# The first two RMS norms of a one-core decoder step: the sum of squares by a stationary of ones, mean and root on every partition

## The chip, the core and the metric

The kernel runs on one core of a Trainium2 chip. The core has a matrix engine (PE, with its weight loads shown apart as PEld), a vector engine (DVE), a scalar engine (ACT), a general engine (POOL) and a queue for transfers (SP). Each works through its own instructions in order and waits on the others through semaphores. The metric is the device time of one execution in microseconds. The kernel before takes 1652.54 us, the median of 3 runs (1651.92 to 1653.86). The kernel keeps a matmul's contraction on the 128 partitions; results land in PSUM banks, all other data lie in SBUF.

## The reference

One layer of a hybrid decoder is computed for 256 prompt tokens and 32 sample tokens together (288 columns, D = 2048 features, 16 blocks of 128 on the partitions):

```
def rmsnorm(x, g):
    y = x32 * lax.rsqrt(jnp.mean(x32 * x32, axis=-1, keepdims=True) + RMS_EPS)
    return y * g

h = rmsnorm(x, norm_mix);  z = h @ w_in             # norm 1, then the input projections
x = x + mixer(z) @ w_out                            # RG-LRU branch and attention branch
x = x + conv_ffn(rmsnorm(x, norm_ffn))              # norm 2, then gate, up, conv, gelu, down
y = rmsnorm(x, norm_final)                          # norm 3
```

In the kernel the features are the partitions and the tokens the columns, so a norm's sum over features runs across partitions, and its root is one number for each column, needed on every partition.

## The kernel before

**Tiling and order.** Nearly all of the work is weight matrices of 128 x 128 against 288 token columns. `unit` (line 181) makes one output block of 128 features: it takes one to three weight tiles from `load_w`, eight 128 x 128 blocks in each, and for every block `mm3` (lines 177 to 179) issues three matmuls, high part by high part, high by low, low by high. A unit of two tiles is 48 matmuls. The program is written in the order in which it runs: no scheduler moves anything (the schedule is manual), and each engine gets its instructions in program order. `load_w` keeps three weight tiles split ahead: each split is an ACT copy that rounds (line 159) and a DVE subtraction (line 160), and there are three buffers for the parts and four for the raw tiles. Units write to one of two PSUM banks in turn (`psg`), so the first matmul of a unit waits until the unit two before it has been read out of its bank.

**The norms.** The scale of a token is applied after the matmul, on the way out of PSUM, so that the projections can begin before the root is known. Norm 1: squares are summed over the 16 blocks into `acc` (128 partitions x 288); then lines 407 to 426 interleave the norm with the first two units, `qx[0]` and `qx[1]`. Norm 2: `squares` on POOL fills `acc` during the output projection; lines 1121 to 1139 interleave the norm in the same way with the first gate unit `q0` and the first up unit `q1`. The steps of a norm are

- `rms_sum` (line 250): three matmuls with 128 columns of `acc` as the stationary and a single column of ones moving; the sums come out with the tokens on the partitions, one column for each 128 tokens;
- `rms_root` (lines 256 and 258): on DVE times 1/D plus eps, 128 x 3, and on POOL the power -1/2, 128 x 3;
- after one weight tile of the next unit, `rms_bcast` (line 266): three matmuls with a root column spread to 128 columns as the stationary and the identity moving, so that every partition gets the row of roots;
- `rms_rows` (line 271): ACT copies that row of 288 from PSUM to `rb`.

Then DVE multiplies the waiting PSUM banks by `rb`: in norm 1 `xr_out` (lines 378, 379) for `qx[0]`, four blocks of `kv[0]` (line 425) and `xr_out` for `qx[1]`; in norm 2 `ffn_gate` (lines 1084, 1085) for `q0` and, after the convolution (1095), `ffn_up` (1100) for `q1`. Behind the root on POOL stand, in norm 1, two DMA issues (427, 467) and in norm 2 the fills of `u` (1080, 1083). Norm 3, at the end, uses the same helpers and is not touched.

Of the kernel before, what the change touches and what calls it, by code (L numbers as in the profile page):

```python
# [9 lines left out]
F32 = mybir.dt.float32  # L10
# [4 lines left out]
ALU = mybir.AluOpType  # L15
# [3 lines left out]
P = 128  # L19
D = 2048  # L20
# [4 lines left out]
N = NP + NS  # L25
# [9 lines left out]
EPS = 1e-6  # L35
# [52 lines left out]
def body(ctx, tc, a, o):  # L88
    nc = tc.nc
    V, S, G, T = nc.vector, nc.scalar, nc.gpsimd, nc.tensor  # L90
# [5 lines left out]
    tmp = ctx.enter_context(tc.tile_pool(name="tmp", bufs=2))  # L96
    ps = ctx.enter_context(tc.tile_pool(name="ps", bufs=2, space=PSUM))

    def bank(tag, bufs):
        return lambda: ps.tile([P, 512], F32, tag=tag, name="ps_" + tag, bufs=bufs)  # L100

    psg, pss, pst, pso, psb = bank("g", 2), bank("s", 2), bank("t", 1), bank("o", 1), bank("b", 2)
# [78 lines left out]
    def unit(out, n, xh, xl):  # L181

        for i in range(n):
            wh, wl = load_w()
            for k in range(8):
                kk = 8 * i + k
                mm3(out, wh[:, k], wl[:, k], xh[:, kk], xl[:, kk], kk == 0, kk == 8 * n - 1)
            if i < n - 1:
                yield
# [20 lines left out]
    ones = cst.tile([P, P], F32, name="ones")  # L210
    V.memset(ones, 1.0)
    mhalf = cst.tile([P, 4], F32, name="mhalf")
# [30 lines left out]
    def new_acc():  # L243
        acc = tmp.tile([P, 384], F32, tag="cv", name="acc")
        V.memset(acc[:, N:], 0.0)
        return acc

    def rms_sum(q, acc, first, last):
        for tb in range(3):
            T.matmul(q[:, tb:tb + 1], acc[:, tb * P:(tb + 1) * P], ones[:, 0:1], start=first and tb == 0, stop=last,  # L250
                     skip_group_check=True)

    def rms_root(q):

        ms = tmp.tile([P, 4], F32, tag="ms", name="ms", bufs=1)
        V.tensor_scalar(ms[:, :3], q[:, :3], 1.0 / D, EPS, op0=ALU.mult, op1=ALU.add)
        rt = tmp.tile([P, 4], F32, tag="rt", name="rt", bufs=1)
        G.tensor_tensor(rt[:, :3], ms[:, :3], mhalf[:, :3], op=ALU.pow)
        return rt

    def rms_bcast(rt):

        q = pss()
        for tb in range(3):
            n = min(P, N - tb * P)
            T.matmul(q[:, tb * P:tb * P + n], rt[:, tb:tb + 1].to_broadcast([P, P]), ident[:, :n], start=True, stop=True)
        return q

    def rms_rows(q):
        rb = tmp.tile([P, N], F32, tag="rb", name="rb", bufs=1)  # L270
        S.activation(rb, q[:, :N], AF.Copy)
        return rb
# [10 lines left out]
    acc = new_acc()  # L283
# [80 lines left out]
    rb = None  # L364
# [12 lines left out]
    def xr_out(j, q):  # L377
        V.tensor_mul(xr[:, j, 3:3 + NP], q[:, :NP], rb[:, :NP])
        V.tensor_mul(xs[:, j, :, 3:], ptok(q[:, NP:N]), ptok(rb[:, NP:]))
# [27 lines left out]
    qn = pss()  # L407
# [4 lines left out]
    r_lam0()  # L412
    for _ in g:
        pass
    rms_sum(qn, acc, True, True)
    rt = rms_root(qn)
    g = unit(qx[1][:, :N], 2, hh, hl)
    next(g)
    qb = rms_bcast(rt)
    for _ in g:  # L420
        pass
    rb = rms_rows(qb)
    xr_out(0, qx[0])
    for j in range(4):
        V.tensor_mul(kv[0][:, j], kz[j][:, :N], rb)
# [630 lines left out]
    acc = new_acc()  # L1056
# [20 lines left out]
    def ffn_gate(f, qg):  # L1077
        u = tmp.tile([P, FW], F32, tag="sx", name="u", bufs=2)
        us = u[:, 2 + NP:].rearrange("p (b t) -> p b t", t=2 + TS)
        G.memset(u[:, 0:2], 0.0)  # L1080
        if 8 <= f < 8 + NB:
            nc.gpsimd.dma_start(o["win"][f - 8], a["win"][f - 8])
        G.tensor_copy(us[:, :, 0:2], fst[:, f].rearrange("p (b t) -> p b t", t=2))
        V.tensor_mul(u[:, 2:2 + NP], qg[:, :NP], rb[:, :NP])  # L1084
        V.tensor_mul(us[:, :, 2:], ptok(qg[:, NP:N]), ptok(rb[:, NP:]))  # L1085
        cv = tmp.tile([P, FW], F32, tag="cv", name="cv")
        S.activation(cv[:, :FC], u[:, 2:2 + FC], AF.Identity, scale=vcol(V_FW + 96, f), bias=vcol(V_FB, f))  # L1087
        G.tensor_copy(fco[:, f, 0:2], u[:, NP:NP + 2])  # L1088
        G.tensor_copy(fco[:, f, 2:18].rearrange("p (b t) -> p b t", t=2), us[:, :, TS:TS + 2])
        late.append(lambda: ffn_conv(f, u, cv))  # L1090
        return cv
# [32 lines left out]
    flush()  # L1124
    for _ in g:
        pass
    qn = pst()
    rms_sum(qn, acc, True, True)
    rt = rms_root(qn)
    q1 = psg()  # L1130
    g = unit(q1[:, :N], 2, h2h, h2l)
    next(g)
    qb = rms_bcast(rt)
    for _ in g:
        pass
    rb = rms_rows(qb)
    cv = ffn_gate(0, q0)
    flush()
    ffn_up(0, q1, cv)
# [13 lines left out]
    acc = new_acc()  # L1153
# [10 lines left out]
    qn = pst()  # L1164
    rms_sum(qn, acc, True, False)
    rms_sum(qn, ex, False, True)
    wake(psg(), 5)
    rt = rms_root(qn)
    q = rms_bcast(rt)
    rb = rms_rows(rms_bcast(rt))  # L1170

# [106 lines left out]
```

## Time and profile before

| what | value |
|---|---|
| median of 3 runs | 1652.54 us (1651.92 to 1653.86) |
| the profiled execution | 1652.34 us |
| its span, first to last instruction | 1650.6 us |
| PE busy | 1639.1 us, 99% |
| DVE, ACT, POOL busy | 994.5, 777.7, 201.4 us |

The span leaves 1.7 us of the profiled execution outside it. A busy PE is not a PE at its peak, since a matmul's end is modelled and overlaps the next; what counts on PE is the distance from one start to the next. The chain of waits follows the work that ended last back to the start.

### The profile page before, as it was taken

The page shows a single profiled execution, that of the slowest core. Times are in us where ns is not written, and L with a number is a line of the kernel's source. Part 1 is how long each engine was busy: PE and PEld are TensorE (multiplying, and loading weights), DVE is VectorE, ACT ScalarE, POOL GpSimd, SP SyncE. Part 2 cuts the span into 40 slices and gives each one's busy share as a digit, 9 for nine tenths or more (in the row PEclk, how much of TensorE's full clock was granted, in tenths as well). Part 3 has the DMA queues.
Part 4 walks back from the last instruction along what each step waited for, and adds up shares of the span by engine and source line. Part 5 has one row for each costly group of instructions (what it writes and reads, how often), then busy time and mean ns, then how long its engine had stood idle before and what let it go on. Part 6 is the DMA issues. An engine that isn't in the chain of part 4 may idle for free.

```text
span 1650.6 us, 31453 instructions
## 1 busy us (share of the span) xinstructions
PE 1639.1 (99%) x12738; PEld 1631.9 (99%) x12738; DVE 994.5 (60%) x1540; ACT 777.7 (47%) x1125; POOL 201.4 (12%) x406
## 2 busy tenths in 40 slices
PE   9999999999999999999999999999999999999997
PEld 9999999999999999999999999999999999999997
DVE  7777776776665555656555656444465556564443
ACT  6566464676754444434444444333344444443332
POOL 1341100421210002330010000000000000001111
PEclk9999999999999999999999999999999999999999
DMA  8655585555565555555576655555555555555553
GB/s 283 180 167 157 166 289 180 147 176 157 175 229 163 173 167 166 168 165 157 175 216 205 180 171 163 177 166 166 165 165 170 165 167 171 172 173 173 162 172 107
DMA packets 89298, 290.78 MB, mean 176 GB/s; under 512 B 10386, under 2 KB 20498, under 8 KB 89026
## 3 DMA queue, kind: packets, MB, share of 16 engines
q1 hardware_dynamic: 86114, 277.00, 55.3%
q0 software_dynamic: 1888, 10.32, 2.0%
q8 instruction: 100, 1.64, 0.4%
q10 hardware_dynamic: 1152, 1.45, 0.3%
q14 instruction: 44, 0.36, 0.1%
HBM read 284.02 MB, written 8.85 MB: 177 GB/s over the span
## 4 chain that ended last, share of the span: by engine, by line
PE 95%; issue 2%; DVE 1%; DMA 1%; POOL 0%; ACT 0%; SPq 0%; ACTq 0%; DVEq 0%; POOLq 0%
PE ps_g L177 30%; PE ps_g L179 30%; PE ps_g L178 30%; PE ps_b L607 1%; PE ps_o L843 0%; DMA kt<-in_slk_dram 0%; DVE wl L160 0%; PE ps_s L828 0%; PE ps_t L834 0%; PE ps_b L957 0%; DVE x L1175 0%; DMA raw<-in_wkc_dram 0%; PE ps_b L177 0%; PE ps_b L179 0%; PE ps_b L178 0%
## 5 line engine op out<-in xcount | busy, mean ns | idle before, releaser
L160 DVE TENSOR_TENSOR wl<-raw,wh 128x1024 fp32r<-128x1024 f32 (+1 forms) x496 | 619.1, 1249 | 463.9 <-ACT wh L159 462.6
L159 ACT ACTIVATE wh<-raw 128x1024 fp32r<-128x1024 f32 (+1 forms) x496 | 522.7, 1054 | 372.7 <-PE ps_g L178 284.3
L177 PE MATMUL ps_g<-h2h,wh 128*128 128x288 f32 x1536 | 450.3, 293 | 0.0
L178 PE MATMUL ps_g<-h2l,wh 128*128 128x288 f32 x1536 | 450.1, 293 | 0.0
L179 PE MATMUL ps_g<-h2h,wl 128*128 128x288 f32 x1536 | 449.4, 293 | 0.0
L177 PE MATMUL ps_g<-hh,wh 128*128 128x288 f32 x1024 | 304.2, 297 | 0.1
L178 PE MATMUL ps_g<-hl,wh 128*128 128x288 f32 x1024 | 300.3, 293 | 0.0
L179 PE MATMUL ps_g<-hh,wl 128*128 128x288 f32 x1024 | 299.8, 293 | 0.0
L179 PEld LDWEIGHTS ps_g<-h2h,wl 128*128 128x128 f32 x1536 | 288.8, 188 | 0.0
L178 PEld LDWEIGHTS ps_g<-h2l,wh 128*128 128x128 f32 x1536 | 288.3, 188 | 0.0
L177 PEld LDWEIGHTS ps_g<-h2h,wh 128*128 128x128 f32 x1536 | 288.3, 188 | 0.0
L177 PE MATMUL ps_g<-gh,wh 128*128 128x288 f32 x768 | 225.0, 293 | 0.0
L178 PE MATMUL ps_g<-gl,wh 128*128 128x288 f32 x768 | 225.0, 293 | 0.0
L179 PE MATMUL ps_g<-gh,wl 128*128 128x288 f32 x768 | 224.7, 293 | 0.0
L177 PEld LDWEIGHTS ps_g<-hh,wh 128*128 128x128 f32 x1024 | 192.3, 188 | 0.7 <-issue 0.4
L178 PEld LDWEIGHTS ps_g<-hl,wh 128*128 128x128 f32 x1024 | 192.3, 188 | 0.3
L179 PEld LDWEIGHTS ps_g<-hh,wl 128*128 128x128 f32 x1024 | 192.5, 188 | 0.0
L179 PEld LDWEIGHTS ps_g<-gh,wl 128*128 128x128 f32 x768 | 144.4, 188 | 0.0
L178 PEld LDWEIGHTS ps_g<-gl,wh 128*128 128x128 f32 x768 | 144.2, 188 | 0.0
L177 PEld LDWEIGHTS ps_g<-gh,wh 128*128 128x128 f32 x768 | 144.1, 188 | 0.0
L1088 POOL COPY fco<-u 128x2 f32<-128x2 f32 x48 | 8.8, 184 | 712.0 <-DVE u L1084 712.0
L1087 ACT ACTIVATE cv<-u,vec 128x304 f32<-128x304 f32 x48 | 30.8, 642 | 132.4 <-DVE u L1085 132.4
(327 smaller groups left out, 2016.4 us busy)
## 6 DMA issues: line engine op xcount, KB each, us to landing
raw<-in_wg_dram SPq DMA_DIRECT2D x96, 512.0 KB, 3.6
raw<-in_wu_dram SPq DMA_DIRECT2D x96, 512.0 KB, 4.1
raw<-in_wd_dram SPq DMA_DIRECT2D x96, 512.0 KB, 3.7
raw<-in_wga_dram SPq DMA_DIRECT2D x32, 512.0 KB, 3.8
raw<-in_wgb_dram SPq DMA_DIRECT2D x32, 512.0 KB, 3.6
raw<-in_wo_dram SPq DMA_DIRECT2D x32, 512.0 KB, 3.6
raw<-in_wxr_dram SPq DMA_DIRECT2D x16, 512.0 KB, 3.7
raw<-in_wgr_dram SPq DMA_DIRECT2D x16, 512.0 KB, 3.7
```

The costliest lines, as they stand in the source:

```text
L159: S.activation(hi, src, AF.Copy)
L160: eng.tensor_sub(lo, src, hi.bitcast(F32))
L177: T.matmul(out, wh, xh, start=first, stop=False)
L178: T.matmul(out, wh, xl, start=False, stop=False)
L179: T.matmul(out, wl, xh, start=False, stop=last)
L607: T.matmul(pc[:, 2 * k:2 * k + 272], w[:, l], f(x), start=lh == 0 and k == 0 and l == 0 and n == 0, stop=lh == 1 and k == 1 and l == 7 and ...
L1087: S.activation(cv[:, :FC], u[:, 2:2 + FC], AF.Identity, scale=vcol(V_FW + 96, f), bias=vcol(V_FB, f))
L1088: G.tensor_copy(fco[:, f, 0:2], u[:, NP:NP + 2])
```

## The change

A new helper, `rms_all`, takes the place of `rms_sum`, `rms_root`, `rms_bcast` and `rms_rows` in norms 1 and 2. One matmul has a 128 x 128 block of ones as the stationary and all of `acc` moving, 288 columns, so each partition receives the sum for every token. DVE then does times 1/D plus eps on 128 x 288 out of PSUM, and POOL takes the power on 128 x 288 straight into `rb`, with the exponent read from one column that is repeated.

```
+    def rms_all(q, acc):
+        T.matmul(q[:, :N], ones, acc[:, :N], start=True, stop=True)
+        ms = tmp.tile([P, N], F32, tag="th", name="msr")
+        V.tensor_scalar(ms, q[:, :N], 1.0 / D, EPS, op0=ALU.mult, op1=ALU.add)
+        rb = tmp.tile([P, N], F32, tag="rb", name="rb", bufs=1)
+        G.tensor_tensor(rb, ms, mhalf[:, 0:1].to_broadcast([P, N]), op=ALU.pow)
+        return rb
...
-    rms_sum(qn, acc, True, True)
-    rt = rms_root(qn)
+    rb = rms_all(qn, acc)
     g = unit(qx[1][:, :N], 2, hh, hl)
     next(g)
-    qb = rms_bcast(rt)
     for _ in g:
         pass
-    rb = rms_rows(qb)
     xr_out(0, qx[0])
...
-    qn = pst()
-    rms_sum(qn, acc, True, True)
-    rt = rms_root(qn)
+    rb = rms_all(pst(), acc)
     q1 = psg()
     g = unit(q1[:, :N], 2, h2h, h2l)
     next(g)
-    qb = rms_bcast(rt)
     for _ in g:
         pass
-    rb = rms_rows(qb)
     cv = ffn_gate(0, q0)
```

On PE in norm 1, between the units `qx[0]` and `qx[1]` (`ps_s` is the norm's bank, `ps_g` a unit's; a name with a number after "waits" is the engine's or transfer's semaphore):

```order
 L178 MATMUL ps_g<-hl,wh 128x288
 L179 MATMUL ps_g<-hh,wl 128x288
-L250 MATMUL ps_s<-ones,acc 128x1 [waits DVE_49]
-L250 MATMUL ps_s<-ones,acc 128x1 x2
+L263 MATMUL ps_s<-acc,ones 128x288 [waits DVE_49]
 L177 MATMUL ps_g<-hh,wh 128x288 [waits Activation_49]
 L178 MATMUL ps_g<-hl,wh 128x288
```

Three matmuls of one column became one of 288 columns. Half-way through `qx[1]`:

```order
 L178 MATMUL ps_g<-hl,wh 128x288
 L179 MATMUL ps_g<-hh,wl 128x288
-L266 MATMUL ps_s<-cs,rt 128x128 [waits DMAHW2_49,Pool_49]
-L266 MATMUL ps_s<-cs,rt 128x128
-L266 MATMUL ps_s<-cs,rt 128x32
 L177 MATMUL ps_g<-hh,wh 128x288 [waits Activation_49]
 L178 MATMUL ps_g<-hl,wh 128x288
```

The three matmuls that spread the roots are gone, and with them PE's own wait for POOL. On DVE in norm 1, before (`wl` are splits of coming weight tiles, `xr` and `kv` the read-outs):

```order
L256 TENSOR_SCALAR ms<-ps_s 128x3 [waits PE_49]
L160 TENSOR_TENSOR wl<-raw,wh 128x1024 [waits DMAHW5_49,Activation_49]
L160 TENSOR_TENSOR wl<-raw,wh 128x1024 [waits DMAHW6_49,PE_49,Activation_49]
L378 TENSOR_TENSOR xr<-ps_g,rb 128x256 [waits Activation_49]
L379 TENSOR_TENSOR xr<-ps_g,rb 128x8x4
L425 TENSOR_TENSOR kv_426<-ps_b,rb 128x288 x2
```

and after:

```order
L265 TENSOR_SCALAR msr<-ps_s 128x288 [waits PE_49]
L160 TENSOR_TENSOR wl<-raw,wh 128x1024 [waits DMAHW5_49,Activation_49]
L160 TENSOR_TENSOR wl<-raw,wh 128x1024 [waits DMAHW6_49,PE_49,Activation_49]
L387 TENSOR_TENSOR xr<-ps_g,rb 128x256 [waits Pool_49]
L388 TENSOR_TENSOR xr<-ps_g,rb 128x8x4
L431 TENSOR_TENSOR kv_426<-ps_b,rb 128x288 x2
```

The places are the same; the mean became 288 columns wide, and the first read-out now waits for POOL instead of ACT. Norm 2 reads alike on both engines, with `u` in the place of `xr`.

## Rows read from the trace of the kernel before

**Rows 1.** The page: busy time of each engine, share of the span, instructions

```profile
PE 1639.1 (99%) x12738; PEld 1631.9 (99%) x12738; DVE 994.5 (60%) x1540; ACT 777.7 (47%) x1125; POOL 201.4 (12%) x406
```

**Rows 2.** The page: the chain that ended last, shares of the span by engine

```profile
PE 95%; issue 2%; DVE 1%; DMA 1%; POOL 0%; ACT 0%; SPq 0%; ACTq 0%; DVEq 0%; POOLq 0%
```

**Rows 3.** Timeline, PE, norm 1: start us, us, engine, line, operation, tiles, shapes, count

```profile
37.75 0.72 PE L250 MATMUL ps_s<-ones,acc 128*128 128x1 f32 x6
...
38.55 0.30 PE L178 MATMUL ps_g<-hl,wh 128*128 128x288 f32 x1
...
41.58 0.75 PE L266 MATMUL ps_s<-cs,rt 128*128 128x128 f32 x6
...
42.39 0.29 PE L178 MATMUL ps_g<-hl,wh 128*128 128x288 f32 x1
...
45.42 0.29 PE L177 MATMUL ps_g<-hh,wh 128*128 128x288 f32 x1
```

**Rows 4.** Timeline, PE, in the attention stage: plain f32 matmuls 256 columns wide

```profile
452.69 0.60 PE L828 MATMUL ps_s<-kv,q_sb 128*128 128x256 f32 x2
...
453.26 0.29 PE L178 MATMUL ps_g<-hl,wh 128*128 128x288 f32 x1
```

**Rows 5.** Timeline, DVE, norm 1 (in brackets: idle before, and who ended it)

```profile
38.51 0.16 DVE L256 TENSOR_SCALAR ms<-ps_s 128x3 f32<-128x3 f32 x1 [0.78 <-PE ps_s L250]
...
42.79 1.23 DVE L160 TENSOR_TENSOR wl<-raw,wh 128x1024 fp32r<-128x1024 f32 x1 [2.61 <-ACT wh L159]
43.94 0.42 DVE L378 TENSOR_TENSOR xr<-ps_g,rb 128x256 f32<-128x256 f32 x1
44.27 0.18 DVE L379 TENSOR_TENSOR xr<-ps_g,rb 128x32 f32<-128x32 f32 x1
```

**Rows 6.** Timeline, ACT, norm 1: the copy of the roots

```profile
42.66 0.40 ACT L271 ACTIVATE rb<-ps_s 128x288 f32<-128x288 f32 x1
```

**Rows 7.** Timeline, DVE, norm 2

```profile
736.36 0.16 DVE L256 TENSOR_SCALAR ms<-ps_t 128x3 f32<-128x3 f32 x1 [1.47 <-PE ps_t L250]
...
741.73 0.42 DVE L1084 TENSOR_TENSOR u<-ps_g,rb 128x256 f32<-128x256 f32 x1
742.07 0.18 DVE L1085 TENSOR_TENSOR u<-ps_g,rb 128x32 f32<-128x32 f32 x1
...
744.04 0.45 DVE L1100 TENSOR_TENSOR t<-ps_g,rb 128x288 f32<-128x288 f32 x1
...
745.73 1.23 DVE L160 TENSOR_TENSOR wl<-raw,wh 128x1024 fp32r<-128x1024 f32 x1 [0.42 <-ACT wh L159]
```

**Rows 8.** Groups of POOL by line and shape: busy us, mean ns | idle before

```profile
L872 POOL TENSOR_TENSOR rest<-kt,k 128x512 f32<-128x512 f32 x32 | 38.6, 1206 | 123.3 <-ACT k L171 104.8 <-DVE k L174 12.8 <-DVE mx L799 2.2
...
L1050 POOL TENSOR_TENSOR m<-m,mA 128x288 f32<-128x288 f32 x16 | 12.9, 809 | 136.7 <-DVE m L1049 128.1 <-DVE acc L245 8.6
...
L258 POOL TENSOR_TENSOR rt<-ms,mhalf 128x3 f32<-128x3 f32 x3 | 2.6, 875 | 22.6 <-DVE ms L256 22.6
...
L767 POOL TENSOR_TENSOR pcs<-pcs,t 128x128 f32<-128x128 f32 x2 | 0.8, 400 | 34.0 <-DVE t L765 34.0
```

**Rows 9.** Timeline, POOL, norm 1 (first row) and norm 2

```profile
38.83 0.85 POOL L258 TENSOR_TENSOR rt<-ms,mhalf 128x3 f32<-128x3 f32 x1 [8.99 <-DVE ms L256]
...
736.60 0.89 POOL L258 TENSOR_TENSOR rt<-ms,mhalf 128x3 f32<-128x3 f32 x1 [4.15 <-DVE ms L256]
...
737.50 0.58 POOL L1083 COPY u<-fst 128x16 f32<-128x16 f32 x1
...
742.50 0.20 POOL L1083 COPY u<-fst 128x16 f32<-128x16 f32 x1
```

**Rows 10.** Timeline, PE: the same matmul at the start and at the end

```profile
1.07 4.21 PE L277 MATMUL ps_g<-ones 128*128 128x128 f32 x18 [1.07 <-DVE mhalf L213]
...
1638.79 1.36 PE L277 MATMUL ps_g<-ones 128*128 128x128 f32 x10
```

**Rows 11.** Stretches: us, busy of PE, PEld, DVE, ACT, POOL, granted clock, DMA share, GB/s

```profile
1642.00:1650.00 8.00, 0.00 (x0) 0.00 (x0) 3.60 (x7) 0.11 (x1) 2.30 (x3) 0.70 0.83 295
```

## The prediction

> **What bounds the kernel now.** I read the page first, then the chain of waits, then the two norms engine by engine. PE is busy for 99% of the span [rows 1] and is 95% of the chain that ended last [rows 2]: the kernel is a single file of matmuls. So an edit is worth what it takes out of PE's file, less any hole it opens there; work on DVE, ACT and POOL is free as long as PE doesn't wait for it. In the timeline of PE around norm 1 the reader is to see starts, not durations: 23 matmuls lie between the starts at 42.39 and 45.42 us, so one costs PE 0.132 us [rows 3].
>
> PE does not wait in either norm today. The first read-out that needs the roots starts at 43.94 us and its second half ends at 44.27 + 0.18 = 44.45 us [rows 5]; the unit that needs the bank it empties starts at 45.42 us [rows 3]. There is about 1 us to spare.
>
> **What comes out of PE's file.** `rms_sum` costs 38.55 - 37.75 = 0.80 us from its first start to the start of the second unit matmul behind it, with one unit matmul in between: 0.80 - 0.13 = 0.67 us for six instructions (each plain f32 matmul is two). `rms_bcast` in the same way: 42.39 - 41.58 - 0.13 = 0.68 us [rows 3]. Together 1.35 us a norm.
>
> **What goes in.** One plain f32 matmul 288 columns wide. Before has none of that width with these operands; the nearest is the pair 256 columns wide in the attention stage: 453.26 - 452.69 - 0.13 = 0.44 us [rows 4], so 0.44 x 288/256 = 0.50 us. Its bounds are 0.44 and the 0.67 of the six instructions. PE gains 1.35 - 0.50 = 0.85 us a norm (0.68 to 0.91), 1.7 us for both. That is 0.1% of the kernel, and it is all that the change can gain: ACT's copy of 0.40 us [rows 6] lies beside PE's work, as does the wider mean on DVE.
>
> **What it opens: the chain to the roots.** In norm 1 the sum would start on PE at 37.75 us as before and take 0.50. The mean started 38.51 - 37.75 = 0.76 us after the six instructions' first start [rows 3, 5], so it now starts at about 38.4 us. Its 128 x 288 out of PSUM costs about 0.45 us (the nearest DVE pass of that width from PSUM [rows 7]) in place of 0.16 [rows 5], so it ends at about 38.9; POOL's power started 0.16 us after the mean's end (38.51 + 0.16 = 38.67 to 38.83 [rows 5, 9]), so the power starts at about 39.0 us. Call its time D. Then comes the read-out, 0.51 us as before, and a tenth for the semaphore. PE needs the bank at 45.42 - 0.85 = 44.57 us. So **the hole in PE is D - 5.0 us**, none if D is below 5.0. Norm 2 has the same steps over the same 48 matmuls (mean at 736.36, read-out 741.73 to 742.25 [rows 7]), so the same hole.
>
> **What is D?** The trace has no power 288 columns wide, so it is bounded from both sides.
>
> - Below: other two-operand POOL passes take 809 ns at 288 columns [rows 8]. If a power is no dearer than these, D = 0.81 us.
> - Above: the power itself takes 875 ns for three columns [rows 8], in all three places alike (0.85 and 0.89 us in the first two [rows 9]). Lines through the other passes, 400 ns at 128 columns, 809 at 288, 1206 at 512, leave 0.08 to 0.30 us at three columns; I take 0.2. So 0.675 us are the power's own, 225 ns a column if all of it goes by columns: D = 0.2 + 288 x 0.225 = 65 us.
> - Between: part of the 0.675 may be paid once. The row just behind the power shows such a cost: the same 16-column copy takes 0.58 us there and 0.20 us on its next turn [rows 9]. With 0.38 us paid once, 0.295 us are left, 98 ns a column: D = 0.2 + 0.38 + 28.2 = 28.8 us.
>
> I take 29 us: the row with the power in it is nearer than any row of another operation, and the one-off is shown beside it, if on another instruction.
>
> What is queued behind: on DVE all read-outs and the next weight split, on POOL two transfers and two fills, which the read-outs' own shift covers. PE is held by the bank alone; the two tiles of the unit that it waits to start are split ahead of the waiting read-out on DVE.
>
> **The clock.** After a hole PE may restart slower. At the start of the kernel 18 of the warm-up instructions take 4.21 us, at the end ten take 1.36 [rows 10]: 4.21 - 18 x 0.136 = 1.8 us lost, roughly the 1.2 level against 2.4 GHz. With no matmul at all the granted clock averages 0.70 [rows 11], so it does fall in a hole. I add 1.8 us a hole, 0 to 1.8 being the bounds.
>
> **Sum**, against the profiled execution of 1652.3 us (the median of the runs is 0.2 above it): -1.7 for PE, +2 x 24 for the holes, +3.6 for the clock: 1652.3 - 1.7 + 48 + 3.6 = **1702 us**.
>
> **Rivals.**
>
> - *The cover holds* (not slower). D is under 5 us, so the power ends before PE wants the bank. Then the read-out waits for the second weight split in front of it, which ends at 42.79 + 1.23 = 44.0 us [rows 5] and moves up with PE, and all that is left is PE's gain: 1650.6 us, "same". It decides at 5.0/288 = 17 ns a column; up to D = 7.5 us the time stays within 0.2%. For it: the other passes' 809 ns. Against it: 875 ns for three columns, which would have to be a fixed cost almost whole. The Trainium skill speaks for this rival (GPSIMD Engine Reference, "Elementwise — side-by-side cycle accounting"): it states about 2.6 cycles an element for an elementwise pass with two operands, measured on an add; by that rule the power would take an estimated 0.6 us plus its dispatch, and the time would be 1650.6 us. The rows of add and multiply agree with it; the row of the power, 875 ns for three columns, does not fit it.
> - *The full price.* All 225 ns go by columns, D = 65 us: 1650.6 + 2 x 60 + 3.6 = 1774 us. For it: the three powers cost the same though the engine did different work before each. Against: the copy's one-off.
> - *A second wait behind the first.* DVE holds the later weight splits behind the read-out, so PE could run dry again after it restarts. In norm 2 the first split behind it ends at 745.73 + 1.23 = 746.96, 4.7 us after the read-out's end at 742.25 [rows 7], and PE then has a unit of 48 x 0.132 = 6.3 us in hand. Price nothing; 1702 stands. It would decide at 1.6 us more on DVE or ACT.
> - *Faster.* PE would have to lose more than 3.3 us of work; both norms hold only 2.7 us of it.
>
> **How the numbers follow.** About 0.2% (3.3 us) is what a measurement of this kernel can tell from no change. The cover holds: 0.30. The forecast, a column price from about 50 to 160 ns: 0.47. The full price: 0.20. Faster: 0.03, for something unseen. So slower 0.67, same 0.30, faster 0.03. The range runs from the case in which the cover holds, 1650, to the full price, 1774; beyond it lie a power dearer than its own row and a faster kernel. The likeliest case's own range is from half its column price (D = 15: 1650.6 + 20 + 3.6 = 1674) to the full price, 1674 to 1774.
>
> **What would show it.** In the profile after, POOL's row for the power 128 x 288 decides: under 5 us the cover holds, about 29 us is my forecast, about 65 the full price. PE should be idle twice, each time ended by DVE's first read-out, and for D - 5.0 us; a hole much unlike that means the five microseconds of cover are wrong. The sum's matmul should take PE 0.5 us. If the power is short and PE still idles, the weight splits are at fault, and the reasoning about DVE's queue is wrong.

## The result and the profile after

The changed kernel takes **1739.07 us**, the median of 4 runs (1738.86 to 1740.52), against 1652.53 us for the kernel before: a ratio of 1.0526, 95% interval 1.0513 to 1.0539. It is 86.5 us slower. The forecast was slower at 1702 us, in a range of 1650 to 1774 us.

The page of the changed kernel answers to [rows 1, 2]: busy time of the engines, the granted clock in 40 slices, and the chain that ended last by engine and by line.

```profile
PE 1641.2 (94%) x12718; PEld 1633.3 (94%) x12718; DVE 996.0 (57%) x1540; ACT 777.2 (45%) x1123; POOL 295.1 (17%) x406
...
PEclk9599999999999999996999999999999999999999
...
PE 90%; POOL 6%; issue 2%; DVE 1%; ACT 1%; DMA 0%; ACTq 0%; DVEq 0%; SPq 0%; POOLq 0%
```

PE does nearly the same work as before (1641.2 us against 1639.1 [rows 1]), but its share fell from 99% to 94%. POOL, which had no share of the chain, now has 6% of it; its busy time grew by 93.7 us. Two slices of the clock dropped, at the two norms. Who made PE wait (engine, line, waited for, us in total, times, longest) and POOL's power in the two norms:

```profile
PE ps_g L177 <- DVE u L1091: 42.3, 1, 42.3
PE ps_g L177 <- DVE xr L388: 42.3, 1, 42.3
```

```profile
38.78 47.30 POOL L267 TENSOR_TENSOR rb<-msr,mhalf 128x288 f32<-128x288 f32 x1 [8.16 <-DVE msr L265]
...
780.29 47.34 POOL L267 TENSOR_TENSOR rb<-msr,mhalf 128x288 f32<-128x288 f32 x1 [4.37 <-DVE msr L265]
...
827.64 0.19 POOL L1089 COPY u<-fst 128x16 f32<-128x16 f32 x1
```

The power takes 47.3 us in place of 0.88 [rows 8, 9], and PE is idle for 42.3 us at each norm. DVE and PE in norm 1 show how one follows from the other; the rows of before are [rows 5] and [rows 3].

```profile
38.24 0.46 DVE L265 TENSOR_SCALAR msr<-ps_s 128x288 f32<-128x288 f32 x1 [0.70 <-PE ps_s L263]
38.77 1.23 DVE L160 TENSOR_TENSOR wl<-raw,wh 128x1024 fp32r<-128x1024 f32 x1
42.41 1.23 DVE L160 TENSOR_TENSOR wl<-raw,wh 128x1024 fp32r<-128x1024 f32 x1 [2.42 <-ACT wh L159]
86.11 0.42 DVE L387 TENSOR_TENSOR xr<-ps_g,rb 128x256 f32<-128x256 f32 x1 [42.48 <-POOL rb L267]
86.46 0.18 DVE L388 TENSOR_TENSOR xr<-ps_g,rb 128x32 f32<-128x32 f32 x1
```

```profile
37.56 0.65 PE L263 MATMUL ps_s<-acc,ones 128*128 128x288 f32 x2
...
38.17 0.29 PE L178 MATMUL ps_g<-hl,wh 128*128 128x288 f32 x1
...
44.21 0.29 PE L179 MATMUL ps_g<-hh,wl 128*128 128x288 f32 x1
86.78 0.58 PE L177 MATMUL ps_g<-hh,wh 128*128 128x288 f32 x1 [42.28 <-DVE xr L388]
87.16 0.44 PE L178 MATMUL ps_g<-hl,wh 128*128 128x288 f32 x1
...
91.00 0.37 PE L179 MATMUL ps_g<-hh,wl 128*128 128x288 f32 x1
91.22 0.29 PE L177 MATMUL ps_g<-hh,wh 128*128 128x288 f32 x1
```

DVE splits two weight tiles and then stands at the first read-out until the power ends at 86.1 us. The read-out ends at 86.64, and PE, which ran out at 44.5, starts 0.14 us later. The sum itself is cheap: 38.17 - 37.56 - 0.13 = 0.48 us on PE. And PE restarts slowly: 18 matmuls from 86.78 to 91.22 us, 4.44 us where 18 x 0.132 = 2.4 would do, so 2.1 us more are lost. Behind the hole of norm 2 it is 1.7 us: 15 matmuls in 3.65 us, where 2.0 would do.

```profile
828.33 0.58 PE L177 MATMUL ps_g<-h2h,wh 128*128 128x288 f32 x1 [42.31 <-DVE u L1091]
...
831.98 0.30 PE L177 MATMUL ps_g<-h2h,wh 128*128 128x288 f32 x1
```

The stretches of norm 1 say why (us, busy of PE, PEld, DVE, ACT and POOL, granted clock, share and rate of transfers):

```profile
37.60:44.60 7.00, 6.91 (x51) 6.57 (x50) 2.91 (x3) 2.31 (x3) 5.82 (x1) 1.00 0.52 151
44.60:88.00 43.40, 1.22 (x5) 1.25 (x6) 1.89 (x6) 0.87 (x1) 41.48 (x1) 0.53 0.04 12
88.00:90.00 2.00, 2.00 (x10) 2.00 (x9) 1.96 (x6) 0.00 (x0) 1.35 (x2) 0.50 0.13 53
```

The clock column reads 1.00 (2.4 GHz) up to the hole and 0.53 on average in it, and in the 2 us after it 0.50, which is the 1.2 GHz level. The transfers nearly stop too (12 GB/s); the longest single wait of the transfer queue, 47.4 us, is for a weight split on DVE. Each norm costs its hole and the slow restart and gives back what PE no longer does, 1.35 - 0.48 = 0.87 us: 2 x (42.3 - 0.87) + 2.1 + 1.7 = 86.7 us, against the 86.5 measured.

### The profile page after: what moved, and what is told of

Same layout as the page of the kernel before. It is cut to its first block, busy times and chain, and to the rows that moved or that the text cites. A ratio compares the mean times of both kernels' runs of the same rounds, so it can differ in the third digit from the quotient of the medians.

```text
span 1737.2 us, 31409 instructions
## 1 busy us (share of the span) xinstructions
PE 1641.2 (94%) x12718; PEld 1633.3 (94%) x12718; DVE 996.0 (57%) x1540; ACT 777.2 (45%) x1123; POOL 295.1 (17%) x406
## 4 chain that ended last, share of the span: by engine, by line
PE 90%; POOL 6%; issue 2%; DVE 1%; ACT 1%; DMA 0%; ACTq 0%; DVEq 0%; SPq 0%; POOLq 0%
PE ps_g L177 28%; PE ps_g L179 28%; PE ps_g L178 28%; POOL rb L267 5%; PE ps_b L613 1%; PE ps_o L849 0%; DVE wl L160 0%; PE ps_s L834 0%; PE ps_t L840 0%; PE ps_b L963 0%; DVE x L1177 0%; DMA raw<-in_wkc_dram 0%; PE ps_b L179 0%; PE ps_b L177 0%; PE ps_b L178 0%
## 5 line engine op out<-in xcount | busy, mean ns | idle before, releaser
L177 PE MATMUL ps_g<-h2h,wh 128*128 128x288 f32 x1536 | 451.2, 294 | 42.3 <-DVE u L1091 42.3
L177 PE MATMUL ps_g<-hh,wh 128*128 128x288 f32 x1024 | 305.2, 298 | 42.4 <-DVE xr L388 42.3
```

The lines of the kernel that those rows point to most:

```text
L177: T.matmul(out, wh, xh, start=first, stop=False)
```

## The experiments

The theory after the result: POOL's power is paid by the column, the 5 us of cover are as read before, and nothing else in the change costs. The rivals: a large fixed cost, the repeated operand, or the wide sum, mean and wait themselves.

**Few columns of the power.** The same kernel, with POOL taking the power of the first columns only and DVE copying the means of the rest: 16, 144, and later 40 columns.

```
-        G.tensor_tensor(rb, ms, mhalf[:, 0:1].to_broadcast([P, N]), op=ALU.pow)
+        G.tensor_tensor(rb[:, :16], ms[:, :16], mhalf[:, 0:1].to_broadcast([P, 16]), op=ALU.pow)
+        V.tensor_copy(rb[:, 16:], ms[:, 16:])
```

> The changed kernel, but POOL takes the power of the first 16 of the 288 columns only; DVE copies the means of the other 272 into the roots' row (so the norms of those tokens are left out). Theory, the power is paid by the column: a line through the old row (875 ns at 3 columns) and the new one (47318 ns at 288) gives 163 ns a column and 0.39 us once, so 0.39 + 16 x 0.163 = 3.0 us, below the 5.0 us of cover; PE has no hole at either norm and the time is that of before less PE's gain of 0.85 us a norm, 1650.8 us. Rival, the wide sum, the wide mean or the new wait on POOL hold PE up by themselves: a hole of some us stays at each norm and the time stays above 1655 us.

Measured: 1650.6 us against 1652.36, ratio 0.9990 (0.9980 to 0.9999). PE waits at neither norm. POOL's two rows of that kernel, the new power and the untouched one of the last norm:

```profile
L267 POOL TENSOR_TENSOR rb<-msr,mhalf 128x16 f32<-128x16 f32 x2 | 6.1, 3036 | 13.7 <-DVE msr L265 13.7
L258 POOL TENSOR_TENSOR rt<-ms,mhalf 128x3 f32<-128x3 f32 x1 | 0.9, 879 | 9.4 <-DVE ms L256 9.4
```

Without the long power all that remains of the change is a gain of 1.76 us. PE's timeline has the same: from one matmul of the units ahead of norm 1 to the same one behind it (35.65 and 142.61 us in the kernel before) this run takes 0.88 us less, and around norm 2 0.89. The wide sum, the wide mean and the wait cost nothing.

> The same with 144 columns on POOL (the power of the other half is left out). Theory, by the column: 0.39 + 144 x 0.163 = 23.9 us for the power, a hole of 23.9 - 5.0 = 18.9 us at each norm, 1.9 us a hole for the clock, so 1650.8 + 2 x 20.8 = 1692 us. Rival, the power has a large cost for any wide row and little by the column: the power near 47 us as before and the time near 1739 us.

Measured: 1692.34 us, ratio 1.0242 (1.0225 to 1.0259). The power and PE's holes:

```profile
L267 POOL TENSOR_TENSOR rb<-msr,mhalf 128x144 f32<-128x144 f32 x2 | 46.7, 23374 | 12.0 <-DVE msr L265 12.0
```

```profile
PE ps_g L177 <- DVE u L1092: 18.4, 1, 18.4
PE ps_g L177 <- DVE xr L389: 18.3, 1, 18.3
```

Half the columns, half the time: the power is paid by the column. Five widths lie within 0.5 us of one line, 0.88 us at 3 columns, 3.04 at 16, 6.87 at 40, 23.37 at 144 and 47.32 at 288. The four slopes between neighbours are 159 to 166 ns a column; the line through the first and the last has 163, with 0.39 us paid once. The time of the run came out as expected by two misses that cancel: the holes are half a microsecond shorter than the 18.9 us expected, and on PE's timeline 2.9 and 2.1 us are lost behind them, where 1.9 was taken.

**Another operation in the same place.** Multiplication for the power, on the same operands.

```
-        G.tensor_tensor(rb, ms, mhalf[:, 0:1].to_broadcast([P, N]), op=ALU.pow)
+        G.tensor_tensor(rb, ms, mhalf[:, 0:1].to_broadcast([P, N]), op=ALU.mult)
```

> The changed kernel with a multiplication in the place of the power on POOL, all 288 columns, same operands and places (the root is left out, so every norm's values differ). Theory, the operation is what costs: POOL's pass takes about 0.8 us like its other passes of this width, no hole, 1650.8 us. Rival, the operand that repeats one column or the place in POOL's queue costs: the pass stays tens of us long and the time near 1739 us.

Measured: 1650.65 us, ratio 0.9989 (0.9979 to 0.9998). The pass takes 1.7 us, where 0.8 was expected, and PE does not wait at the norms.

```profile
L267 POOL TENSOR_TENSOR rb<-msr,mhalf 128x288 f32<-128x288 f32 x2 | 3.5, 1734 | 13.7 <-DVE msr L265 13.7
```

So the operation is what costs, not the place, the width or the operands. The pass's double time is taken up again in the last section.

**A written-out exponent.** The exponent as 288 columns in memory, not one column read 288 times.

```
+        mf = tmp.tile([P, N], F32, tag="sx", name="mf", bufs=2)
+        V.memset(mf, -0.5)
...
-        G.tensor_tensor(rb, ms, mhalf[:, 0:1].to_broadcast([P, N]), op=ALU.pow)
+        G.tensor_tensor(rb, ms, mf, op=ALU.pow)
```

> The changed kernel with the exponent written out over 288 columns, in the place of one column that is repeated. Theory, the power is paid by the column whatever it reads: 47.3 us, holes of 42.3 us, 1739 us. Rival, reading one column 288 times is what is slow: the power falls well below 47 us and the time falls with it by twice that.

Measured: 1739.34 us, ratio 1.0527 (1.0509 to 1.0545), and the same power:

```profile
L269 POOL TENSOR_TENSOR rb<-msr,mf 128x288 f32<-128x288 f32 x2 | 94.9, 47454 | 12.2 <-DVE msr L267 12.2
```

The repeated operand is not the cause.

**Close to the edge of the cover.** Forty columns.

> The changed kernel with 40 columns of the power on POOL (the other 248 get their means, the power is left out there). Theory, 5.0 us of cover and 163 ns a column: the power takes 0.39 + 40 x 0.163 = 6.9 us and leaves a hole of 1.9 us at each norm, 1650.8 + 3.8 = 1654.6 us, or up to 1658 if so short a hole costs the clock as much as the long ones did. Rival, the cover is a microsecond longer or shorter than read from before: the hole is 0.9 or 2.9 us.

Measured: 1656.68 us (1655.16 to 1658.16), ratio 1.0027 (1.0015 to 1.0038). The power takes 6.87 us and the holes are 1.8 and 1.9 us:

```profile
PE ps_g L177 <- DVE u L1092: 1.9, 1, 1.9
PE ps_g L177 <- DVE xr L389: 1.8, 1, 1.8
```

The cover is 6.87 - 1.82 = 5.05 us here, 23.37 - 18.33 = 5.04 with 144 columns, 47.30 - 42.28 = 5.02 in the change. The time is about 2 us above the 1654.6 that the holes alone give, within what was allowed for the clock; the last section comes back to it.

**One norm alone.** The second norm changed, the first as before (the first part of the diff undone).

```
-    rb = rms_all(qn, acc)
+    rms_sum(qn, acc, True, True)
+    rt = rms_root(qn)
...
+    qb = rms_bcast(rt)
...
+    rb = rms_rows(qb)
```

> Only the second norm is changed, the first is that of before. Theory, two holes of their own: one hole of 42.3 us and 2.0 us for the clock less 0.85 us, 1652.5 + 43.4 = 1696 us. Rival, part of the loss of one norm is given back or comes again elsewhere in the kernel: more than 3 us away from 1696 us.

Measured: 1696.66 us (1696.12 to 1696.82), ratio 1.0267 (1.0251 to 1.0283). That is 44.3 us for norm 2 alone, and about what was expected: nothing large is given back elsewhere. The 42.4 us left over for norm 1 are a difference of two runs and not its own cost. PE has the same hole of 42.3 us at norm 2 here as in the change, but behind it 24 matmuls, from 785.11 to 790.94 us, take 5.8 us where 3.2 would do: 2.7 us are lost, not 1.7.

**Another root.** The sum by ones and the mean of the change, with a square root on ACT and a reciprocal on DVE.

```
-        G.tensor_tensor(rb, ms, mhalf[:, 0:1].to_broadcast([P, N]), op=ALU.pow)
+        S.activation(ms, ms, AF.Sqrt)
+        V.reciprocal(rb, ms)
```

> The changed kernel with the power replaced: a square root on ACT, in place on the means, and a reciprocal on DVE into the roots' row; sum by ones and mean as in the change. Theory, the place of the root is free as long as it ends within the 5 us of cover: a table load of 1.28 us and a pass of about 0.45 us on ACT, a reciprocal of about 0.5 us or a few times that on DVE, about 3 us in all, no hole, 1650.8 us, 0.1% below before. Rival, the extra table load or the queue of weight splits behind it on ACT makes PE wait: a hole of 1 us or more at a norm, at or above the time of before.

Measured: 1651.89 us against 1652.40, ratio 0.9997 (0.9988 to 1.0006): no difference is shown, and the 1650.8 us expected lie inside the interval too. PE has no hole at either norm, so the rival falls. ACT, DVE and PE in norm 1:

```profile
36.98 1.28 ACT L267 ACT_TABLE_LOAD   x1
39.41 0.45 ACT L267 ACTIVATE msr<-msr 128x288 f32<-128x288 f32 x1 [1.14 <-DVE msr L265]
```

```profile
39.88 1.95 DVE L268 RECIPROCAL rb<-msr 128x288 f32<-128x288 f32 x1 [0.51 <-ACT msr L267]
...
43.39 1.23 DVE L160 TENSOR_TENSOR wl<-raw,wh 128x1024 fp32r<-128x1024 f32 x1 [0.47 <-ACT wh L159]
```

```profile
44.88 0.29 PE L179 MATMUL ps_g<-hh,wl 128*128 128x288 f32 x1
45.20 0.37 PE L177 MATMUL ps_g<-hh,wh 128*128 128x288 f32 x1
```

The table load lies ahead of the mean, beside other work. The reciprocal is the long one, 1.95 us, and pushes the splits and the read-out to the edge of the cover. The root then fits in, but with nothing to spare: PE starts the next unit 0.32 us after the matmul before it, where 0.13 is the pace.

**One pass fewer.** Mean and square root in one ACT pass out of PSUM.

```
+    epst = cst.tile([P, 1], F32, name="epst")
+    V.memset(epst, EPS)
...
-        V.tensor_scalar(ms, q[:, :N], 1.0 / D, EPS, op0=ALU.mult, op1=ALU.add)
+        S.activation(ms, q[:, :N], AF.Sqrt, scale=1.0 / D, bias=epst)
...
-        G.tensor_tensor(rb, ms, mhalf[:, 0:1].to_broadcast([P, N]), op=ALU.pow)
+        V.reciprocal(rb, ms)
```

> The changed kernel with mean and root in one pass on ACT, straight out of PSUM (square root with the scale 1/D and eps as bias), and the reciprocal on DVE: one DVE pass of 0.46 us and one hand-over fewer than with the mean on DVE. In that run the first unit after norm 1 started 0.32 us after the matmul before it, where 0.13 is the pace, since the reciprocal took 1.95 us and pushed the weight splits and the read-out back. Theory: with about 0.5 us less in the chain that gap goes, and all of PE's gain is kept, 1650.7 us, 0.1% below before. Rival: ACT's pass out of PSUM comes behind a weight split in its queue and gains nothing: about 1651.9 us, no difference from before.

Measured: 1651.47 us against 1653.07 beside it, ratio 0.9992 (0.9983 to 1.0001). The interval still holds 1, and the gap before the next unit is there as in the run before:

```profile
44.47 0.29 PE L179 MATMUL ps_g<-hh,wl 128*128 128x288 f32 x1
44.78 0.37 PE L177 MATMUL ps_g<-hh,wh 128*128 128x288 f32 x1
```

```profile
42.98 1.23 DVE L160 TENSOR_TENSOR wl<-raw,wh 128x1024 fp32r<-128x1024 f32 x1 [0.92 <-ACT wh L159]
```

The start-to-start distance is 0.31 us again. Shortening the chain did not close the gap, so the theory missed that part; the read-out still comes behind the second weight split, for which DVE waits 0.92 us on ACT. What kept ACT from starting it sooner the trace doesn't name. No version's time was shown to beat the kernel before by more than the comparison can tell. On PE's timeline, between the same matmuls as in the sixteen-column run, both versions with the square root take 0.6 us less than before around norm 1 and 0.9 around norm 2, so the gap costs some 0.25 us at norm 1 alone. The bound on such a version is the gain of the sixteen-column and the multiplication runs, 1.7 us or 0.1%.

## Why the prediction came out as it did

- **What bounds the kernel, and what PE gains.** Right. 0.85 us a norm was worked out; the sum costs 0.48 where 0.50 was taken, and the sixteen-column run puts both norms at 1.76 us against 1.7.
- **The hole is D - 5.0 us.** Right at three widths: 5.02, 5.04 and 5.05 us of cover.
- **D.** This is the term that was mis-sized. 29 us was taken between 0.8 and 65; it is 47.3, and the loss of 50 us that was forecast came out at 86.5. The step that failed is the one-off: 0.38 us of the power's 875 ns [rows 8] were set down as paid once *besides* the 0.2 us that any pass costs, on the strength of the copy behind the power, 0.58 against 0.20 us [rows 9]. In the changed kernel the same copy behind a far longer power takes 0.19 us, so its slowness does not come from the power; it ran beside a weight split on DVE (last section). The five widths give 0.39 us paid once in all, and (875 - 390)/3 = 162 ns a column, where 98 was taken and 225 was the upper bound. No row that was read could tell a fixed cost of 0.39 us from 0.2 or 0.58: the plain pass's 0.2 alone gives 65 us, as far above as the forecast lay below. That the time still fell into the range is owed to its width, up to the full price; the case that carried the forecast's chance, 50 to 160 ns a column, was just missed.
- **The rival in which the cover holds** fell with D. The rule of the Trainium skill that spoke for it (GPSIMD Engine Reference, "Elementwise — side-by-side cycle accounting": about 2.6 cycles an element for a pass with two operands, measured on an add) does not hold for the power: the estimate worked out from it was 0.6 us for 288 columns besides the dispatch, and the power took 47.3. The multiplication in its place took 1.73 us beside a weight split; the other passes of that width take 0.81 us [rows 8]. **The full price** was nearer than the forecast in form, since almost all is by the column, but its fixed part was too small.
- **The clock.** 1.8 us a hole was added; 2.1 us were lost behind the first and 1.7 behind the second. The upper bound of 1.8 was too low: 1.6 to 2.9 us were lost behind the holes of all the runs. With D = 47.3 the sum of the prediction reads 1650.6 + 2 x 42.3 + 3.6 = 1738.8 us, and 1739.07 was measured: with D put right the other terms close the sum.
- **A second wait behind the first.** Rightly priced at nothing: PE's waits at the norms are the two holes alone, and the sum closes to within 0.3 us.

## What to carry to other kernels

An operation measured on a few columns says little about a wide one until its cost is split into what is paid once and what is paid by the column; one row can't give that split, and a one-off seen on another instruction doesn't either. A second width does: the rows at 3 and 16 columns put 288 at 0.88 + 285 x 0.166 = 48.2 us, where 47.3 was measured. A broadcast that looks like waste can be what keeps an expensive operation narrow: here three roots a partition and a 0.68 us broadcast on PE replace 288 powers on each partition. And an engine off the critical path is free only up to its cover, which here was read from the trace before the change was made, 5.0 us against the 5.02 to 5.05 measured.

## What the runs showed of the hardware

**The power on POOL** costs 163 ns a column of 128 partitions; at 288 columns that is 27 times the multiplication in its place (1.73 us). The exponent may be one repeated column or written out: 47.32 and 47.45 us. All runs have the exponent -1/2.

**A short hole costs the clock after the restart.** At norm 1 of the forty-column run PE restarts at 46.37 us at its full pace after a hole of 1.8 us and keeps it for some ten matmuls; then it slows. From PE's timeline and the stretches of that run (columns as above):

```profile
46.37 0.37 PE L177 MATMUL ps_g<-hh,wh 128*128 128x288 f32 x1 [1.82 <-DVE xr L389]
46.58 0.29 PE L178 MATMUL ps_g<-hl,wh 128*128 128x288 f32 x1
...
47.68 0.44 PE L177 MATMUL ps_g<-hh,wh 128*128 128x288 f32 x1
47.92 0.44 PE L178 MATMUL ps_g<-hl,wh 128*128 128x288 f32 x1
```

```profile
44.40:47.00 2.60, 0.78 (x7) 0.66 (x6) 1.29 (x5) 1.06 (x1) 1.27 (x1) 1.00 0.71 202
47.00:50.00 3.00, 3.00 (x17) 3.00 (x16) 2.88 (x9) 0.00 (x0) 1.35 (x2) 0.60 0.23 94
50.00:52.00 2.00, 2.00 (x14) 2.00 (x13) 1.67 (x11) 0.78 (x1) 0.00 (x0) 0.75 0.91 210
```

The granted clock reads 1.00 during the hole and 0.60 and 0.75 in the two stretches behind it, with PE busy throughout: on PE's timeline 1.6 us are lost there. At norm 2 of the same run it fell sooner, and the third matmul already is a slow one; again 1.6 us are lost:

```profile
747.03 0.37 PE L177 MATMUL ps_g<-h2h,wh 128*128 128x288 f32 x1 [1.86 <-DVE u L1092]
...
747.39 0.45 PE L179 MATMUL ps_g<-h2h,wl 128*128 128x288 f32 x1
```

The price of a hole of under 2 us is thus nearly twice its length in this profile; by the medians of the runs, (1656.68 - 1650.6) / 2, it is 3.0 us. And the loss behind a hole doesn't grow with its length in these runs: 1.6 us twice behind 1.8 us, 2.9 and 2.1 behind 18.3, 2.1, 1.7 and (norm 2 alone) 2.7 behind 42.3.

**Passes of POOL and DVE at the same time.** The multiplication took 1.73 us while DVE ran a weight split that began at the same moment:

```profile
40.07 1.73 POOL L267 TENSOR_TENSOR rb<-msr,mhalf 128x288 f32<-128x288 f32 x1 [9.36 <-DVE msr L265]
```

```profile
40.05 1.23 DVE L160 TENSOR_TENSOR wl<-raw,wh 128x1024 fp32r<-128x1024 f32 x1
```

A pass of this width takes 0.81 us elsewhere [rows 8]. The trace of before shows when. The same add of 128x288 (line 241) runs 29 times: 15 times it starts while a split is running on DVE and takes 1.66 to 1.68 us, 14 times DVE is idle and it takes 0.80 to 0.81. The add of line 1050 starts ahead of a split 16 times and keeps its 0.81 us, and there it is the split that takes longer, in most places 1.48 us in place of 1.23. One of each:

```profile
730.78 1.66 POOL L241 TENSOR_TENSOR acc<-acc,sq 128x288 f32<-128x288 f32 x1
...
1628.95 0.81 POOL L241 TENSOR_TENSOR acc<-acc,sq 128x288 f32<-128x288 f32 x1
```

```profile
730.51 1.27 DVE L160 TENSOR_TENSOR wl<-raw,wh 128x1024 fp32r<-128x1024 f32 x1 [0.55 <-ACT wh L159]
```

```profile
572.77 0.81 POOL L1050 TENSOR_TENSOR m<-m,mA 128x288 f32<-128x288 f32 x1 [8.63 <-DVE m L1049]
```

```profile
573.18 1.48 DVE L160 TENSOR_TENSOR wl<-raw,wh 128x1024 fp32r<-128x1024 f32 x1 [0.56 <-ACT wh L159]
```

In all of these rows the one of the two that starts second pays. The slow copy of before, at 737.50 us [rows 9], also started inside a split (736.80 to 738.03 us), and the quick ones at 827.64 us and in the sixteen-column run did not. The power is another matter: the two splits that run beside it in norm 1 keep their 1.23 us. No run varied this by itself.
